# A hybrid decoder step: attention scores from 32-row products, another order of the projection's column groups, low halves of weights by an adding transfer

## The chip, the core and the metric

The kernel runs on one core of one Trainium2 chip. The metric is the device time of one launch in microseconds (us). Engines are named as in the profile: PE (TensorE, matmuls), DVE (VectorE), ACT (ScalarE), POOL (GpSimd), SP (the engine that issues most DMAs).

## What is computed

Two layers, each a mixing sub-layer and a feed-forward sub-layer, for 512 prompt rows and 32 sample rows (8 sequences of 4, over a paged cache of 2048 keys). All in float32. Cut from the reference, the mixing sub-layer:

```
P = rms_norm(x, g) @ w_in          # 1024 -> 2048: a, gate, u, v(sgu), q, k, v, d: 256 columns each
A: h = a*sigmoid(gate); causal depthwise conv, width 31; LayerNorm; silu        -> ya
B: u * (tril(W_s) @ (LN(v)*g + b) + b_s), chunks of 128, 4 heads (gelu on u, v)  -> yb
C: 4 heads, two softmax maps each of 32-wide keys/queries with ALiBi:
   p = softmax(q1 k1' + bias) - lam * softmax(q2 k2' + bias);  p @ v; RMSNorm    -> yc
D: means over windows 2/4/8/16 minus the token, a linear map per group           -> yd
x = x + rms_norm([ya yb yc yd] @ w_out)
```

## The kernel before

**Exact products.** Float32 products are made of three reduced-precision ones: every operand is split into a rounded high part and the rest, and hi·hi, lo·hi and hi·lo are accumulated. For a block of weights the high part `whi` is an ACT copy (L190) of the raw block, and the low part `wlo` is a DVE subtraction (L193), 128 x 1024 each. `whi` and `wlo` have rings of four slots, the raw blocks of 1 MB (256 columns) two.

**The projection.** `mixing` (L348) is run once a layer. It goes through eight column groups in the order of the table `order`; each is two chunks of 128 columns, and each chunk is done in two parts, the first 256 prompt rows and then 256 more with the 32 sample rows (288), 24 matmuls a part (8 blocks of the inner dimension times three products). `LAG` = 2: the second part of a chunk is written two steps after its first. So a layer has 8 x 2 x 2 x 24 = 768 such matmuls. The order before is a, gate, k, q, v, d, u, v of the gating: columns 0, 256, 1280, 1024, 1536, 1792, 512, 768.

**The mixers** are Python generators that are advanced between the projection's steps:

- `conv` with `taps` (A): once `gate` is there, DVE makes h (L410, tile `hext`) and then 31 instructions of 128 x 512 for each of the two chunks (L413 and 30 times L416, tile `cacc`), 60 at L416 a layer; then a LayerNorm over transposed tiles, a tanh, and the split into `ya` (L345 on ACT, L346 on DVE).
- `attention` (C): for each of two chunks 8 units, each with two score maps of width W = 128, 256, 384 or 512. Score products need k and q stacked as hi, lo, hi against hi, hi, lo in 96 rows, so that one matmul does all three products. `stack` builds these: a split of k and q (L474 on DVE), and 24 DMAs of 64 KB a chunk on SP (L478). DVE scales and takes the maximum of each map (L501), ACT takes the exponential, DVE makes the factors (L511 reciprocal, L512) and combines both maps (L513), PE transposes (L516) and multiplies with v (tile `oT`). It ends with an RMS norm on POOL and DVE and the split into `yc`.
- `gating` (B): LayerNorm per 128 tokens (L595), times gain (L596) plus offset (L597) as 128 x 256 tiles, and the product with W_s; `pooling` (D) ends with `yd`.

**The output product** (w_out, 192 matmuls of 512 columns in `project_last`) takes its inner blocks in the order `W_OUT_ORDER` = yd, ya, yb, yc. A Tile framework with a scheduler decides the order of the instructions on each engine when the program is built; each engine then runs its list in order.

Of the kernel before, what the change touches and what calls it, by code (L numbers as in the profile page):

```python
# [8 lines left out]
F32 = mybir.dt.float32  # L9
# [8 lines left out]
SEQ = 512  # L18
# [20 lines left out]
PB = 10  # L39
# [81 lines left out]
def trunk(ctx, tc, A, O):  # L121
# [15 lines left out]
    def acc():  # L137
        return psx("acc")
# [12 lines left out]
    ident = cst[:, C_ID:C_ID + 128]  # L151
    selkg = cst[:, C_KG:C_KG + 32]
# [123 lines left out]
    def params(l, tp, bank):  # L276
        lam_init = 0.8 - 0.6 * math.exp(-0.3 * l)
        rows = tp.tile([72, 128], F32, tag="prow", name="prow")
        for i, n in enumerate(("conv_b", "conv_ln_g", "conv_ln_b", "pool_scale")):
            SY.dma_start(rows[2 * i:2 * i + 2, :], A[n][l].rearrange("(c p) -> c p", p=128))  # L280
        SY.dma_start(rows[8:70, :], A["conv_w"][l].rearrange("t (c p) -> (t c) p", p=128))
        for i in range(2):
            SY.dma_start(rows[70:71, 64 * i:64 * i + 64], A["attn_sub_g"][l:l + 1, :])
        o = psx(bank)
        T.transpose(o[:, :71], rows[:71, :], ident[:71, :71])
        pf, lm = PF[l][0], PL[l]
        V.tensor_copy(pf[:, :71], o[:, :71])
        V.tensor_scalar(pf[:, 72:76], pf[:, 2:6], 0.5, None, op0=ALU.mult)
# [59 lines left out]
    def mixing(l, mp, early):  # L348
# [10 lines left out]
        kT, kh, kl, qh, ql = {}, {}, {}, {}, {}  # L359
# [33 lines left out]

        qT = {}
# [28 lines left out]
        def conv():  # L423
# [7 lines left out]
            cn = mp.tile([128, 256], F32, tag="t256", bufs=1, name="cn")  # L431
# [25 lines left out]
        ST = {}  # L457

        def stack():
            for c in range(2):  # L460
                st = ST[c] = {}

                o = ps()
                for t in range(4):
                    T.transpose(o[:, 128 * t:128 * t + 128], kT[c][:, 128 * t:128 * t + 128], ident)
                kt = mp.tile([128, 4, 128], F32, tag="t512", bufs=4, name="ktok")
# [3 lines left out]
                for nm, src, seqs in (("k", kT[c], (0, 1, 0)), ("q", qT[c], (0, 0, 1))):  # L470
                    hi = mp.tile([128, SEQ], F32R, tag="t512", bufs=4, name="qkh")
                    lo = mp.tile([128, SEQ], F32R, tag="t512", bufs=4, name="qkl")
                    S.copy(hi, src)
                    V.tensor_tensor(lo, src, hi.bitcast(F32), op=ALU.subtract)  # L474
                    s = yp.tile([128, 4, SEQ], F32R, tag="y", name=f"st_{nm}")
                    for jj in range(4):
                        for g in range(3):
                            SY.dma_start(s[32 * g:32 * g + 32, jj, :].bitcast(F32), (hi, lo)[seqs[g]][32 * jj:32 * jj + 32, :].bitcast(F32))  # L478
                    st[nm] = s
                    yield  # L480

        def attention():
            pb = mp.tile([128, SEQ], F32, tag="pb", name="pb")
            SY.dma_start(pb, A["c_pbias"])
            y = None
            for c in range(2):
                st = ST[c]
# [5 lines left out]
                def scores(i, hh):  # L493
                    h, W = 2 * c + hh, 128 * (i + 1)
                    P = []
                    for m in range(2):
                        sp = psx("s")
                        mm(sp[:, :W], st["q"][0:96, 2 * hh + m, 128 * i:128 * i + 128], st["k"][0:96, 2 * hh + m, 0:W])
                        p = mp.tile([128, SEQ], F32, tag="p", bufs=PB, name="p")
                        mn = mp.tile([128, 1], F32, tag="mn", bufs=8, name="mn")  # L500
                        V.tensor_tensor_reduce(p[:, :W], sp[:, :W], pb[:, SEQ - W:], SLOPES[h], 3.0e38,  # L501
                                               ALU.add, ALU.min, mn)
                        S.activation(p[:, :W], p[:, :W], AF.Exp, scale=-1.0, bias=mn, accum_out=den[:, i, hh, m:m + 1])
                        P.append(p)
                    Pm[i, hh] = P

                def weights(i, hh):
# [3 lines left out]
                    V.reciprocal(dn[:, 2:3], dn[:, 1:2])  # L511
                    V.tensor_scalar(dn[:, 3:4], dn[:, 0:1], dn[:, 2:3], nlam, op0=ALU.mult, op1=ALU.mult)  # L512
# [15 lines left out]
                for u in range(len(units) + UL):  # L528
                    if u < len(units):
                        scores(*units[u])  # L530
                    if u >= UL:
                        i, hh = units[u - UL]
                        weights(i, hh)
                        if hh == 1:
                            values(i)
                    yield
                os_ = mp.tile([128, SEQ], F32, tag="t512", bufs=4, name="os_")
                sq = mp.tile([128, SEQ], F32, tag="t512", bufs=4, name="sq")
# [12 lines left out]
                rb = mp.tile([128, 4, 2, 64], F32, tag="t512", bufs=4, name="rb")  # L551
# [12 lines left out]
        def gating():  # L564
            wn = mp.tile([128, 4, 128], F32, tag="t512", bufs=4, name="wn")
# [17 lines left out]
            SG[l] = (wc, bc)  # L583
            yield
# [5 lines left out]
            for t in range(4):  # L590
# [5 lines left out]
                V.tensor_tensor(vn[:, t, :], vn[:, t, :], gr[:, 0, :], op=ALU.mult)  # L596
                V.tensor_tensor(vn[:, t, :], vn[:, t, :], gr[:, 1, :], op=ALU.add)  # L597
                yield
            y = yp.tile([128, 2, 2, SEQ], F32R, tag="y", name="yb")
            for c in range(2):  # L600
                o = acc()
                for n in range(4):
                    for hh in range(2):
# [3 lines left out]
                V.tensor_tensor(t, o.rearrange("p (n t) -> p n t", n=4),  # L607
                                bsg[:, c:c + 1, :].to_broadcast([128, 4, 128]), op=ALU.add)
# [9 lines left out]
        def pooling():  # L618
# [7 lines left out]
            cn = mp.tile([128, 256], F32, tag="t256", bufs=1, name="cn")  # L626
# [57 lines left out]
        def load(c0):  # L684
# [4 lines left out]
            else:  # L689
                pairs[c0] = raw_cols(w, c0, V, early.get(c0), None, G if c0 == 0 and early else None)  # L690
# [21 lines left out]
        for u in range(n + LAG):  # L712
# [17 lines left out]
            if b >= 0:  # L730
# [14 lines left out]
                if c0 == 1024 and i == 1:  # L745
                    active.append(stack())
                if i == "v":
                    active.append(attention())
# [635 lines left out]
    with tc.tile_pool(name="pro", bufs=1, reuse_waits="tile") as pro, \  # L1384
# [76 lines left out]
```

## Time and profile before

| | |
|---|---|
| time, median of 3 runs | 1456.01 us (1452.26 to 1457.11) |
| the profiled execution | 1448.71 us, of it 1446.8 us from the first to the last instruction |
| PE, DVE, ACT, POOL busy | 95%, 57%, 35%, 18% of the span |
| the first layer's mixing | 14 to 175 us; its w_out from 175 us |
| the second layer's mixing | 736 to 890 us; its w_out from 890 us |

Busy shares are means over the whole span; the two mixing stages are about a fifth of it, and there DVE is busier than its mean. The granted clock is 1.00 (2.4 GHz) in most stretches and 0.50 (1.2 GHz) in some.

### The profile page before, as it was taken

To read this page: it belongs to the slowest core of one execution; us is meant where nothing else is said; L and a number is where in the kernel's file an instruction comes from. 1 tells how busy PE (TensorE), PEld (TensorE's weight loads), DVE (VectorE), ACT (ScalarE), POOL (GpSimd) and SP (SyncE) were. 2 spreads that over 40 slices of the span, in tenths; PEclk is the share of its full clock that TensorE was granted. 3 is DMA by queue.
4 is the path that set the end of the run, shared out by engine and by line. 5 is a ranking of instruction groups with operands and counts; after the bars stand their busy time and mean duration, and the time that the engine had idled before them with its cause. 6 is when DMAs were issued, how large, how long until landed. Compare 5 with 4: busy or idle time off the path is not lost.

```text
span 1446.8 us, 22864 instructions
## 1 busy us (share of the span) xinstructions
PE 1372.0 (95%) x9114; PEld 1078.7 (75%) x9114; DVE 823.8 (57%) x1660; ACT 504.7 (35%) x985; POOL 262.7 (18%) x271
## 2 busy tenths in 40 slices
PE   6999787999999999999989988989999999999997
PEld 6987576877666777777689976777776677768775
DVE  4986759866434333333669976778663333333344
ACT  4346634322224321222343474543322332222231
POOL 1000145455300000000220011544442000000003
PEclk9999799999999999999999997999999999999999
DMA  6452134888848752132434521468877496213132
GB/s 206 116 156 73 59 121 145 301 307 297 296 164 254 241 171 77 59 117 106 150 120 119 146 68 58 163 237 281 318 276 266 153 315 220 81 61 114 59 135 91
DMA packets 160091, 242.15 MB, mean 167 GB/s; under 512 B 10444, under 2 KB 118226, under 8 KB 159986
## 3 DMA queue, kind: packets, MB, share of 16 engines
q1 hardware_dynamic: 141410, 173.32, 37.1%
q0 software_dynamic: 18432, 67.12, 12.4%
q8 instruction: 72, 1.18, 0.3%
q14 instruction: 33, 0.27, 0.1%
q10 hardware_dynamic: 144, 0.26, 0.0%
HBM read 222.33 MB, written 12.04 MB: 162 GB/s over the span
## 4 chain that ended last, share of the span: by engine, by line
PE 81%; DVE 11%; ACT 2%; DMA 2%; issue 2%; POOL 1%; SPq 1%; DVEq 0%; POOLq 0%; ACTq 0%
PE acc L126 61%; PE sx L126 12%; PE ps L126 3%; DVE sca L872 2%; PE s L126 1%; DVE cacc L416 1%; DVE p L501 1%; DVE wlo L193 1%; DVE m L1301 1%; PE oT L126 1%; DVE x_t L1294 1%; ACT whi L190 1%; PE ps L516 1%; SPq L478 1%; PE ps L1001 1%
## 5 line engine op out<-in xcount | busy, mean ns | idle before, releaser
L126 PE MATMUL acc<-xhi,whi 128*128 128x512 f32 (+2 forms) x1152 | 405.5, 353 | 3.2 <-ACT whi L190 2.0
L126 PE MATMUL acc<-xhi,wlo 128*128 128x512 f32 (+2 forms) x1152 | 403.4, 351 | 0.2 <-DVE wlo L193 0.2
L126 PE MATMUL acc<-xlo,whi 128*128 128x512 f32 (+2 forms) x1152 | 402.0, 349 | 1.3 <-DVE xlo L238 1.3
L190 ACT CAST whi<-raw 128x1024 fp32r<-128x1024 f32 x178 | 184.3, 1048 | 333.7 <-PE acc L126 292.8
L193 DVE TENSOR_TENSOR wlo<-raw,whi 128x1024 fp32r<-128x1024 f32 x172 | 217.1, 1268 | 128.7 <-ACT whi L190 126.8
L126 PEld LDWEIGHTS acc<-xhi,whi 128*128 128x128 f32 x1152 | 217.1, 189 | 42.2 <-issue 8.0
L126 PEld LDWEIGHTS acc<-xlo,whi 128*128 128x128 f32 x1152 | 217.2, 189 | 31.9 <-issue 4.1
L126 PEld LDWEIGHTS acc<-xhi,wlo 128*128 128x128 f32 x1152 | 216.9, 188 | 31.5 <-issue 4.7
L126 PE MATMUL acc<-whi,h 128*128 128x512 f32 x704 | 226.7, 397 | 0.0
L126 PEld LDWEIGHTS acc<-whi,h 128*128 128x128 f32 x704 | 131.2, 188 | 44.1 <-issue 11.1
L126 PE MATMUL acc<-wlo,h 128*128 128x512 f32 x352 | 138.6, 395 | 0.0
L1276 POOL TENSOR_TENSOR m<-m,g_g_ffn_post 128x512 f32<-128x512 f32 x14 | 20.1, 1437 | 504.9 <-ACT junk L1275 504.9
L989 DVE STREAM_TRANSPOSE kt<-kr 128x1024 f32<-128x1024 f32 x64 | 78.5, 1233 | 27.6 <-DMA kr<-in_cache_k_dram,ik 23.3
L986 POOL DMA_INDIRECT kr<-in_cache_k_dram,ik x64 | 73.8, 1154 | 100.1 <-DVE kt L989 72.2
L416 DVE SCALAR_TENSOR_TENSOR cacc<-hext,pf,cacc 128x512 f32<-128x512 f32 x120 | 85.4, 747 | 0.6
L1345 DVE SCALAR_TENSOR_TENSOR th<-th,acc 128x512 f32<-128x512 f32 (+1 forms) x46 | 29.9, 649 | 87.2 <-PE acc L126 87.0
L126 PEld LDWEIGHTS acc<-wlo,h 128*128 128x128 f32 x352 | 66.1, 188 | 17.6 <-issue 4.5
L174 POOL TENSOR_TENSOR rsw<-rsw,mhalf 128x1 f32<-128x1 f32 (+2 forms) x62 | 39.1, 636 | 202.9 <-DVE rsw L173 189.4
L1016 POOL DMA_INDIRECT vr<-in_cache_v_dram,iv x64 | 63.2, 988 | 57.0 <-PE sx L126 41.2
L1154 DVE SCALAR_TENSOR_TENSOR sth<-sth,ps 128x64 f32<-128x64 f32 x22 | 4.8, 220 | 86.5 <-ACT sth L1153 86.5
L550 POOL TENSOR_TENSOR rse<-e,mhalf 128x8 f32<-128x8 f32 x4 | 8.5, 2130 | 242.7 <-DVE e L548 242.7
L126 PE MATMUL sx<-vr,pt 128*32 128x256 f32 x512 | 49.3, 381 | 0.0
(401 smaller groups left out, 1864.8 us busy)
## 6 DMA issues: line engine op xcount, KB each, us to landing
raw<-in_w_gu_dram SPq DMA_DIRECT2D x44, 1024.0 KB
raw<-in_w_down_dram SPq DMA_DIRECT2D x20, 1024.0 KB
rws<-in_w_gu_dram SPq DMA_DIRECT2D x40, 512.0 KB
raw<-in_w_in_dram SPq DMA_DIRECT2D x16, 1024.0 KB
raw<-in_w_out_dram SPq DMA_DIRECT2D x8, 1024.0 KB
rwo<-in_w_out_dram SPq DMA_DIRECT2D x16, 512.0 KB
rws<-in_w_down_dram SPq DMA_DIRECT2D x16, 512.0 KB
x<-x_t SPq DMA_DIRECT2D x12, 512.0 KB
```

What stands on the lines that cost most here:

```text
L126: T.matmul(out, lhsT, rhs, start=start, stop=stop)
L174: G.tensor_tensor(y, v, mhalf[:P, :n], op=ALU.pow)
L190: S.copy(hi, src)
L193: eng.tensor_tensor(lo, src, hi.bitcast(F32), op=ALU.subtract)
L416: V.scalar_tensor_tensor(a, hext[c][:, t:t + SEQ], pf[:, 8 + 2 * t + c:9 + 2 * t + c], a, op0=ALU.mult, op1=ALU.add)
L478: SY.dma_start(s[32 * g:32 * g + 32, jj, :].bitcast(F32), (hi, lo)[seqs[g]][32 * jj:32 * jj + 32, :].bitcast(F32))
L872: V.scalar_tensor_tensor(a[:, c], ext[:, c, :, t:t + 4], pf[:, 8 + 2 * t + c:9 + 2 * t + c], a[:, c], op0=ALU.mult, op1=ALU.add)
L986: G.indirect_dma_start(out=kr, out_offset=None, in_=ck, in_offset=bass.IndirectOffsetOnAxis(ap=ik[:, s, bg:bg + 1], axis=0))
L989: V.transpose(kt, kr)
L1016: G.indirect_dma_start(out=v.rearrange("p t e -> p (t e)"), out_offset=None, in_=cv, in_offset=bass.IndirectOffsetOnAxis(ap=iv[:, s, a:a + ...
L1276: (V if (t, half) == (3, 1) else G).tensor_tensor(m[t][:, hs], m[t][:, hs], gain[:, hs], op=ALU.mult)
L1345: V.scalar_tensor_tensor(th[:, :n], th[:, :n], 0.5, ou[:, :n], op0=ALU.mult, op1=ALU.mult)
```

## The change

- **Order of the groups:** k, q, v first, then a, gate, u, v of the gating, d last. `attention` starts when the first chunk of q is done, and no longer waits for stacks.
- **Scores:** no stacks (48 DMAs, 4 DVE splits and 8 transposes a layer fall away). High and low parts of k and q are made where the projection's result is read (`ev_qk`: 8 DVE instructions of 256 columns a layer instead of 4 of 512), and each map is three accumulated matmuls over 32 rows. The keys go out through 16 small products with a unit matrix.
- **Low halves:** in the five groups a, gate, u, v of the gating and d, ACT writes -raw rounded into `wlo`, a GpSimd DMA that adds in place puts the raw weights on top from memory (512 KB, runs of 512 bytes), and ACT makes `whi`: 10 such transfers a layer in place of 10 DVE subtractions.
- **Small ones:** reciprocals and factors for both maps' units of a pair at once (16 + 16 become 8 + 8); gain and offset of the gating's LayerNorm move behind the product with W_s (8 DVE instructions fewer, four matmuls and one DVE instruction more); `PB` (score tiles) 10 to 8, ring `t512` 4 to 3.

```diff
-PB = 10
+PB = 8
+    identr = cp.tile([128, 128], F32R, name="identr")
+    S.copy(identr, ident)
...
+        qk = {(nm, c): [mp.tile([128, SEQ], F32R, name=f"{nm}{c}{s}") for s in "hl"] for nm in "kq" for c in range(2)}
...
+        def ev_qk(nm, c, f):
             def ev(o, half):
+                hi, lo = qk[nm, c]
                 hs = slice(256 * half, 256 * half + 256)
+                if nm == "k":
+                    S.copy(hi[:, hs], o[:, :256])
+                    V.tensor_tensor(lo[:, hs], o[:, :256], hi[:, hs].bitcast(F32), op=ALU.subtract)
                 else:
+                    sc = cst[:, C_QS + c:C_QS + c + 1]
+                    S.activation(hi[:, hs], o[:, :256], AF.Copy, scale=sc)
+                    V.scalar_tensor_tensor(lo[:, hs], o[:, :256], sc, hi[:, hs].bitcast(F32), op0=ALU.mult, op1=ALU.subtract)
...
         order = [
+            (1280, [(10, ev_qk("k", 0, 10)), (11, ev_qk("k", 1, 11))]),
+            (1024, [(8, ev_qk("q", 0, 8)), (9, ev_qk("q", 1, 9))]),
+            (1536, "v"),
             (0, [(0, ev_copy(hext[0], 0, 0.5, 30)), (1, ev_copy(hext[1], 1, 0.5, 30))]),
             (256, [(2, ev_ga(0)), (3, ev_ga(1))]),
-            (1280, [(10, ev_tmp(kT, 0, 10, "kT")), (11, ev_tmp(kT, 1, 11, "kT"))]),
-            (1024, [(8, ev_tmp(qT, 0, 8, "qT")), (9, ev_tmp(qT, 1, 9, "qT"))]),
-            (1536, "v"),
-            (1792, [(14, ev_copy(dext[0], 14, 1.0, 15)), (15, ev_copy(dext[1], 15, 1.0, 15))]),
             (512, [(4, ev_copy(uv[:, 0], 4)), (5, ev_copy(uv[:, 1], 5))]),
             (768, [(6, ev_copy(uv[:, 2], 6)), (7, ev_copy(uv[:, 3], 7))]),
+            (1792, [(14, ev_copy(dext[0], 14, 1.0, 15)), (15, ev_copy(dext[1], 15, 1.0, 15))]),
         ]
...
+        def keys_out():
             for c in range(2):
                 o = ps()
                 for t in range(4):
+                    for s in range(2):
+                        mm(o[:, 128 * t:128 * t + 128], qk["k", c][s][:, 128 * t:128 * t + 128], identr, start=(s == 0), stop=(s == 1))
...
+                    sps = [psx("s") for _ in range(2)]
+                    for n, (a, b) in enumerate(((0, 0), (0, 1), (1, 0))):
+                        for m in range(2):
+                            r = slice(64 * hh + 32 * m, 64 * hh + 32 * m + 32)
+                            mm(sps[m][:, :W], qk["q", c][a][r, 128 * i:128 * i + 128], qk["k", c][b][r, 0:W], start=(n == 0), stop=(n == 2))
                     for m in range(2):
-                        sp = psx("s")
-                        mm(sp[:, :W], st["q"][0:96, 2 * hh + m, 128 * i:128 * i + 128], st["k"][0:96, 2 * hh + m, 0:W])
+                        sp = sps[m]
...
-                V.tensor_tensor(vn[:, t, :], vn[:, t, :], gr[:, 0, :], op=ALU.mult)
-                V.tensor_tensor(vn[:, t, :], vn[:, t, :], gr[:, 1, :], op=ALU.add)
...
-                pairs[c0] = raw_cols(w, c0, V, early.get(c0), None, G if c0 == 0 and early else None)
+                if c0 in (1280, 1024):
+                    pairs[c0] = raw_cols(w, c0, V, early.get(c0), None, G if c0 == 1280 and early else None)
+                    return
+                r = raw_load(w, c0)
+                pairs[c0] = []
+                for i in range(2):
+                    hi = wp.tile([128, 8, 128], F32R, tag="whi", bufs=4, name="whi")
+                    lo = wp.tile([128, 8, 128], F32R, tag="wlo", bufs=4, name="wlo")
+                    src = r[:, :, 128 * i:128 * i + 128]
+                    S.activation(lo, src, AF.Copy, scale=-1.0)
+                    G.dma_start(lo, w[:, c0 + 128 * i:c0 + 128 * i + 128].rearrange("(k p) f -> p k f", p=128),
+                                accum_op=ALU.add)
+                    S.copy(hi, src)
+                    pairs[c0].append((hi, lo))
...
+                if c0 == 1024:
+                    done.add(("q", i))
+                    if i == 0:
+                        active.append(attention())
+                    else:
+                        active.append(keys_out())
                 if i == "v":
-                    active.append(attention())
+                    done.add("v")
```

How the instructions stand on three engines' lists, in the first layer (numbers behind names tell copies of a tile apart; line numbers are those of each kernel).

DVE, before, where the convolution begins; `wlo` are low halves of weights, `hext` is h, `cacc` the convolution's sum:

```order
L193 TENSOR_TENSOR wlo<-raw,whi 128x1024
L410 SCALAR_TENSOR_TENSOR hext_231<-tg,hext_231 128x512
L296 TENSOR_TENSOR lam_81<-lam_81 128x1
L582 COPY bc_1814<-bsg 128x8
L413 TENSOR_SCALAR cacc_442<-hext_231,pf_82 128x512
L297 TENSOR_SCALAR lam_81<-lam_81 128x1
L416 SCALAR_TENSOR_TENSOR cacc_442<-hext_231,pf_82,cacc_442 128x512 x4
L193 TENSOR_TENSOR wlo<-raw,whi 128x1024
L416 SCALAR_TENSOR_TENSOR cacc_442<-hext_231,pf_82,cacc_442 128x512 x6
```

The same place of the change (`p,mn<-s,pb` is a score map with its maximum):

```order
L499 ISA p,mn<-s,pb 128x256
L499 ISA mn 128x1
L419 SCALAR_TENSOR_TENSOR hext_233<-tg,hext_233 128x512
L499 ISA p,mn<-s,pb 128x256
L499 ISA mn 128x1
L422 TENSOR_SCALAR cacc_1216<-hext_233,pf_84 128x512
L425 SCALAR_TENSOR_TENSOR cacc_1216<-hext_233,pf_84,cacc_1216 128x512
L499 ISA p,mn<-s,pb 128x256
L499 ISA mn 128x1
L425 SCALAR_TENSOR_TENSOR cacc_1216<-hext_233,pf_84,cacc_1216 128x512 x2
```

The first instruction on `hext` stood at row 26 of DVE's list, ahead of all score maps, and stands at row 98, behind 22 of the layer's 32 maps.

DVE, before, the rows around the last low half of `yc`, the last operand of w_out to be made:

```order
L597 TENSOR_TENSOR vn<-vn,sgr 128x256
L607 TENSOR_TENSOR uv<-acc,bsg 128x512 x2
L610 TENSOR_TENSOR uv<-uv 128x512 x2
L346 TENSOR_TENSOR yb<-uv,yb 128x512 x2
L548 SCALAR_TENSOR_TENSOR e_1984<-ps,e_1984 128x8
L552 COPY rb<-rse 128x512
L556 SCALAR_TENSOR_TENSOR os__1975<-os__1975,pf_82,ps 128x512
L346 TENSOR_TENSOR yc<-os__1975,yc 128x512
```

The end of the mixing on DVE in the change:

```order
L350 TENSOR_TENSOR yb<-uv,yb 128x512
L652 TENSOR_TENSOR s_1917<-wn,cst 128x15
L653 SCALAR_TENSOR_TENSOR wn<-wn,cst,dext_236 128x497
L175 TENSOR_SCALAR rsw<-ag 128x1
L655 TENSOR_TENSOR wn<-s_1917,dext_236 128x15
L450 TENSOR_SCALAR xn<-ps,ag,rsw 128x256
L350 TENSOR_TENSOR yd<-wn,yd 128x512
L460 SCALAR_TENSOR_TENSOR cacc_1216<-hext_233,cacc_1216 128x512
L460 SCALAR_TENSOR_TENSOR cacc_1722<-hext_234,cacc_1722 128x512
L350 TENSOR_TENSOR ya<-cacc_1216,ya 128x512
L350 TENSOR_TENSOR ya<-cacc_1722,ya 128x512
```

The last operand to be made was `yc`; now `yc` is made far ahead, and `ya` is the last, right behind `yd` and `yb`.

POOL, before, from the clearing of the convolution's margins on:

```order
L355 MEMSET hext_231 128x30
L356 MEMSET dext_233 128x15
L355 MEMSET hext_232 128x30
L356 MEMSET dext_234 128x15
L550 TENSOR_TENSOR rse<-e_1534,mhalf 128x8
L578 AFFINE_SELECT wt<-wt 128x512
```

And in the change:

```order
L359 MEMSET hext_234 128x30
L360 MEMSET dext_236 128x15
L703 DMA wlo<-in_w_in_dram 128x8x128 x7
L552 TENSOR_TENSOR rse<-e_1084,mhalf 128x8
L703 DMA wlo<-in_w_in_dram 128x8x128 x3
L552 TENSOR_TENSOR rse<-e_1574,mhalf 128x8
```

Ten adding transfers stand on POOL's list, around the first of the two instructions (`rse`) on which attention's norm waits.

## Rows read from the trace of the kernel before

**Rows 1.** The profile page: busy time of the engines, and the chain that ended last.

```profile
PE 1372.0 (95%) x9114; PEld 1078.7 (75%) x9114; DVE 823.8 (57%) x1660; ACT 504.7 (35%) x985; POOL 262.7 (18%) x271
...
PE 81%; DVE 11%; ACT 2%; DMA 2%; issue 2%; POOL 1%; SPq 1%; DVEq 0%; POOLq 0%; ACTq 0%
```

**Rows 2.** Windows: PE, PEld, DVE, ACT, POOL busy (x); PE clock; DMA share, GB/s.

```profile
175.00:188.50 13.50, 12.02 (x64) 9.93 (x60) 5.14 (x10) 3.10 (x6) 2.19 (x3) 1.00 0.03 11
188.50:223.00 34.50, 32.09 (x151) 25.21 (x151) 25.81 (x91) 13.00 (x31) 15.74 (x14) 1.00 0.46 155
223.00:245.00 22.00, 15.92 (x91) 13.55 (x91) 21.87 (x49) 12.41 (x27) 13.67 (x13) 0.84 0.47 152
40.42:122.15 81.73, 78.33 (x606) 74.22 (x604) 76.44 (x153) 37.06 (x93) 0.00 (x0) 1.00 0.46 130
122.15:188.48 66.33, 52.05 (x331) 42.05 (x327) 40.11 (x121) 37.79 (x78) 11.76 (x13) 0.82 0.16 53
149.90:170.40 20.50, 12.68 (x47) 8.20 (x47) 16.37 (x58) 14.98 (x33) 4.00 (x6) 0.50 0.15 52
```

**Rows 3.** DVE's instructions by line, 40.4 to 188.4 us.

```profile
L416 DVE SCALAR_TENSOR_TENSOR cacc<-hext,pf,cacc 128x512 f32<-128x512 f32 x60 | 42.6, 747 | 0.3
L193 DVE TENSOR_TENSOR wlo<-raw,whi 128x1024 fp32r<-128x1024 f32 x15 | 18.6, 1238 | 2.8 <-ACT whi L190 2.7
L501 DVE CUSTOM_DVE_ANT_0 p<-s,pb 128x128 f32<-128x128 f32 (+3 forms) x32 | 14.8, 482 | 1.8 <-PE s L126 1.7
L513 DVE SCALAR_TENSOR_TENSOR p<-p,den 128x128 f32<-128x128 f32 (+3 forms) x16 | 8.4, 543 | 0.1
L512 DVE TENSOR_SCALAR den<-den,lam 128x1 f32<-128x1 f32 x16 | 4.0, 266 | 0.1
...
L596 DVE TENSOR_TENSOR vn<-vn,sgr 128x256 f32<-128x256 f32 x4 | 1.6, 421 | 0.0
...
L474 DVE TENSOR_TENSOR qkl<-kT,qkh 128x512 fp32r<-128x512 f32 x2 | 1.4, 688 | 0.7 <-DMA st_q<-qkh 0.7
```

**Rows 4.** The chain of waits, 36 to 66 us: start, us, what.

```profile
47.43 3.07 PE acc L126 x23
...
59.11 2.65 DVE cacc L416 x4
```

**Rows 5.** DVE's timeline: first gating multiply, a last tap, last low half, both layers.

```profile
40.42 0.68 DVE L410 SCALAR_TENSOR_TENSOR hext<-tg,hext 128x512 f32<-128x512 f32 x1
...
113.39 0.75 DVE L416 SCALAR_TENSOR_TENSOR cacc<-hext,pf,cacc 128x512 f32<-128x512 f32 x1
...
188.48 0.69 DVE L346 TENSOR_TENSOR yc<-os__1975,yc 128x512 fp32r<-128x512 f32 x1 [0.68 <-ACT yc L345]
...
759.62 0.68 DVE L410 SCALAR_TENSOR_TENSOR hext<-tg,hext 128x512 f32<-128x512 f32 x1
...
903.59 0.69 DVE L346 TENSOR_TENSOR yc<-os__8388,yc 128x512 fp32r<-128x512 f32 x1 [0.68 <-ACT yc L345]
```

**Rows 6.** PE's timeline at four places, with what it waited for.

```profile
37.94 0.23 PE L285 MATMUL ps<-cst,prow 71*128 71x71 f32 x1
...
188.50 0.50 PE L126 MATMUL acc<-whi,yc 128*128 128x512 f32 x1 [1.49 <-ACT yc L345]
...
192.29 0.50 PE L126 MATMUL acc<-whi,yd 128*128 128x512 f32 x1 [2.13 <-ACT whi L190]
...
268.49 0.28 PE L126 MATMUL acc<-xhi,whi 128*128 128x256 f32 x1
268.61 0.28 PE L126 MATMUL acc<-xlo,whi 128*128 128x256 f32 x1
268.82 0.53 PE L126 MATMUL sx<-kt,qs 128*32 128x128 f32 x11
```

**Rows 7.** GpSimd's gathering transfers of the paged keys (512 KB each): duration, landing.

```profile
L986 POOL DMA_INDIRECT kr<-in_cache_k_dram,ik x64: 933/941/1936, 252.2 to 1086.2; - x64
...
DMA to landing us min/median/max: 4.2/6.5/9.8
```

More of the change, by code (lines that the diff above doesn't have):

```diff
@@ L277, in params @@
         lam_init = 0.8 - 0.6 * math.exp(-0.3 * l)
-        rows = tp.tile([72, 128], F32, tag="prow", name="prow")
+        rows = tp.tile([74, 128], F32, tag="prow", name="prow")
         for i, n in enumerate(("conv_b", "conv_ln_g", "conv_ln_b", "pool_scale")):
@@ L283, in params @@
             SY.dma_start(rows[70:71, 64 * i:64 * i + 64], A["attn_sub_g"][l:l + 1, :])
+        SY.dma_start(rows[71:73, :], A["sgu_ln_g"][l].rearrange("(c p) -> c p", p=128))
         o = psx(bank)
-        T.transpose(o[:, :71], rows[:71, :], ident[:71, :71])
+        T.transpose(o[:, :73], rows[:73, :], ident[:73, :73])
         pf, lm = PF[l][0], PL[l]
         V.tensor_copy(pf[:, :71], o[:, :71])
+        V.tensor_copy(pf[:, 77:79], o[:, 71:73])
         V.tensor_scalar(pf[:, 72:76], pf[:, 2:6], 0.5, None, op0=ALU.mult)
@@ L358, in mixing @@
         vtok = mp.tile([128, 4, 256], F32, name="vtok")
-        kT, kh, kl, qh, ql = {}, {}, {}, {}, {}
+        qk = {(nm, c): [mp.tile([128, SEQ], F32R, name=f"{nm}{c}{s}") for s in "hl"] for nm in "kq" for c in range(2)}
+        pb = mp.tile([128, SEQ], F32, name="pb")
+        SY.dma_start(pb, A["c_pbias"])
+        done = set()
         tg = {}
@@ L454, in conv @@
             Y[0] = y
-        ST = {}
-        def stack():
+        def keys_out():
             for c in range(2):
-                st = ST[c] = {}
                 o = ps()
                 for t in range(4):
-                    T.transpose(o[:, 128 * t:128 * t + 128], kT[c][:, 128 * t:128 * t + 128], ident)
-                kt = mp.tile([128, 4, 128], F32, tag="t512", bufs=4, name="ktok")
+                    for s in range(2):
+                        mm(o[:, 128 * t:128 * t + 128], qk["k", c][s][:, 128 * t:128 * t + 128], identr, start=(s == 0), stop=(s == 1))
+                kt = mp.tile([128, 4, 128], F32, tag="t512", bufs=3, name="ktok")
                 S.copy(kt, o.rearrange("p (t f) -> p t f", t=4))
@@ L469, in stack @@
                 yield
[L470 to L480, printed above, removed]
         def attention():
-            pb = mp.tile([128, SEQ], F32, tag="pb", name="pb")
-            SY.dma_start(pb, A["c_pbias"])
             y = None
             for c in range(2):
-                st = ST[c]
+                while ("q", c) not in done:
+                    yield
                 oT = psx("oT")
@@ L510, in weights @@
                     dn = den[:, i, hh]
-                    V.reciprocal(dn[:, 2:3], dn[:, 1:2])
-                    V.tensor_scalar(dn[:, 3:4], dn[:, 0:1], dn[:, 2:3], nlam, op0=ALU.mult, op1=ALU.mult)
+                    if hh == 0:
+                        d2 = den[:, i]
+                        V.reciprocal(d2[:, :, 2:3], d2[:, :, 1:2])
+                        V.scalar_tensor_tensor(d2[:, :, 3:4], d2[:, :, 0:1], nlam, d2[:, :, 2:3], op0=ALU.mult, op1=ALU.mult)
                     V.scalar_tensor_tensor(P[0][:, :W], P[1][:, :W], dn[:, 3:4], P[0][:, :W], op0=ALU.mult, op1=ALU.add)
@@ L534, in attention @@
                         if hh == 1:
+                            while "v" not in done:
+                                yield
                             values(i)
                     yield
-                os_ = mp.tile([128, SEQ], F32, tag="t512", bufs=4, name="os_")
-                sq = mp.tile([128, SEQ], F32, tag="t512", bufs=4, name="sq")
+                os_ = mp.tile([128, SEQ], F32, tag="t512", bufs=3, name="os_")
+                sq = mp.tile([128, SEQ], F32, tag="t512", bufs=3, name="sq")
                 S.copy(os_, oT)
@@ L583, in gating @@
             SG[l] = (wc, bc)
+            o = acc()
+            for h in range(4):
+                mm(o[64 * (h % 2):64 * (h % 2) + 64, 128 * (h // 2):128 * (h // 2) + 128], gr[:, 64 * h:64 * h + 64], wt[:, h, :])
+            V.tensor_tensor(bsg, o[:, :256].rearrange("p (c t) -> p c t", c=2), bsg, op=ALU.add)
             yield
@@ L606, in gating @@
                 t = uv[:, 2 + c, :].rearrange("p (n t) -> p n t", n=4)
[L607 to L608 removed]
+                V.scalar_tensor_tensor(t, o.rearrange("p (n t) -> p n t", n=4), pf[:, 77 + c:78 + c],
+                                       bsg[:, c:c + 1, :].to_broadcast([128, 4, 128]), op0=ALU.mult, op1=ALU.add)
                 tf = uv[:, 2 + c, :]
@@ L1391, in trunk @@
         g = grow(pro, "g_mix_pre", 0)
-        early = {0: raw_load(A["w_in"][0], 0)}
+        early = {1280: raw_load(A["w_in"][0], 1280)}
         for t in range(2, 5):
             SY.dma_start(xs[t][:rows_of(t)], x_at(0)(128 * t, rows_of(t)))
-        early[256] = raw_load(A["w_in"][0], 256)
+        early[1024] = raw_load(A["w_in"][0], 1024)
         for t in range(5):
```

26 lines of the change are left out of this document (8 added, 18 removed).

## The prediction

> **What bounds the kernel now.** The page first: PE is busy 95% of the span, and the chain that ended last runs over PE for 81% and over DVE for 11% [rows 1]. Over the whole kernel, a us taken from DVE is therefore worth nothing where PE is full. So the stages have to be looked at one by one, and the windows show three of them in a layer's mixing [rows 2]. From 40.4 to 122.2 us both engines are full (PE 78.3, DVE 76.4 of 81.7 us). From 122.2 to 188.5 neither is (52.1 and 40.1 of 66.3); here the stage waits for chains of small steps, and PE's clock falls to 0.50, its lower level of 1.2 GHz, for 20.5 us in which it is busy for 12.7. Then the output product fills PE again (32.1 of 34.5 us). The timeline shows what releases it: the product's matmul at 188.50 waited for `yc`, whose low half DVE made at 188.48 [rows 5, 6]. So the end of the mixing is set by the mixer that is made last, and a change in this stage is worth what it does to that moment, S. The change makes another mixer last (`ya`), so S has to be built anew: when can the convolution begin (T0), how much DVE work stands from there to the last `ya`, and how much of w_out is left at that moment.
>
> **T0, where the convolution can begin.** Before, DVE multiplies the gate into h at 40.42 [rows 5]. After, `a` and `gate` are the fourth and fifth groups. I counted PE's list: the transpose of the parameters, at 37.94 before [rows 6], has the same 184 matmuls ahead of it in both kernels. Behind it, up to the second part of the gate's first chunk, stand 240 projection matmuls of 256 columns, 120 of 288, 66 of scores (22 maps, three each, 279 columns on average), 16 that bring out keys, and some 40 transposes and products with v. Prices: 0.12 us for 256 columns (268.49 to 268.61, [rows 6]), 0.133 for 288 (23 in 3.07 us, [rows 4]), so 0.46 ns a column. That makes 28.8 + 16.0 + 8.5 + 1.8 + 6.6 (the last an estimate at 0.11 to 0.2 each) = 61.7, and with 0.7 for the tanh on ACT T0 = 37.9 + 61.7 + 0.7 = 100.3. Three corrections:
>
> - A score product uses 32 of the array's rows, and changes its tiling and back. Where the kernel before changes from full size to 32 columns, the next start comes after 0.21 us and not after 0.12 [rows 6]: 0.09 each way. There are 13 bursts before T0: +2.4 us. The Trainium skill (TensorEngine Tiling, Key Properties) says that a change of the tiling mode drains the engine; the trace agrees by these 0.09 us.
> - The two maps of a unit lie in different rows of the array and are written alternately. If such pairs run side by side, half of 8.5 us falls away; if not, nothing. No row of before shows a product of 32 rows. I take half of it, -2.2 us.
> - The adding transfers. No row shows one. Nearest are the gathered keys, of the same size and also issued by POOL: 4.2 to 9.8 us to landing, 6.5 in the middle [rows 7]. Low end 4.2. They move 128 pieces of 4 KB and the adding transfer 1,024 pieces of 512 bytes, so the high end is 9.8 plus seven more issues of 0.94 = 16. Counting on PE's list from the matmul that frees a slot of the ring to the first that reads the new weights, less an ACT pass, the slack is 7.2 us for the first chunk of `a`, 8.7 for the second, 4.9 for the first of the gate. At 6.5 only the last is late, by 1.6 us. The Trainium skill (DMA: Bandwidth & Descriptors, Anatomy of one DMA) gives 2.0 us plus the bytes at 436 KB a us, an estimate of 3.2 us here; the gathered keys take twice that, so I stay with the rows.
>
> T0 = 100.3 + 2.4 - 2.2 + 1.6 = 102, which is 62 us later than before. Ends: 96 and 118.
>
> **DVE from T0 to the last `ya`.** Before, from the first multiply to the last low half, DVE is busy 76.4 + 40.1 = 116.6 us [rows 2]. What of it is gone or lies ahead of T0 in the change (neighbours overlap by 0.08 us: four taps in 2.65 us, 0.66 each against 0.75 by itself [rows 3, 4]; it is taken off each):
>
> - 22 of 32 score maps lie ahead; the ten left have 4,096 of 10,240 columns, so 60% of 14.8 goes, less overlap: 7.1.
> - Ten of 16 combinations (L513) lie ahead; the rest has 45% of the columns: 3.8. Factors: 26 small instructions at 0.19 and half of that: 3.4.
> - 4 low halves of weights are left of 15: 11 x 1.16 = 12.8. Splits of k and q (L474): 2.4. Gain and offset (L596 and its twin): 2.7, less 0.4 for the new addition [rows 3].
>
> Together 31.8, so 85 us stay, in which the 60 taps alone are 40. The relief is real, about 16 us a layer over the whole stage, but before T0 DVE now has only about 38 us of work, and an engine can't catch up later what it was not given earlier. About 65 us of the 85 stand up to the last tap. Taps are always at hand, so this runs between gapless (65) and the 93.5% of the window from 40.4 [rows 2] (69.5); I take 67. The 20 us behind it (pooling, both layer norms, gating, `yd`, `yb`, `ya`) are a chain through PE, POOL, ACT and DVE as in the window from 122.2, where DVE works 60% of the time [rows 2]: 20 if gapless, 33 at that rate. Part of the chain overlaps with the taps; I take 26.
>
> S = 102 + 67 + 26 = 195, against 188.5 before. Ends: 96 + 85 = 181, and 118 + 102 = 220.
>
> **What it costs at the end.** PE is done with the projection some 53 us behind T0 and waits for S, with w_out behind it. Before, 49 of w_out's 192 matmuls had run while it waited (most of the 64 in the window from 175 [rows 2]); from 188.5 on, 143 x 0.23 us (512 columns at 0.46 ns) = 32.9 and a stall of 2.1 at 192.29 [rows 6] ended at 223.5. After the change only six matmuls stand ahead of `ya` in PE's list: 186 x 0.23 = 42.8, and 195 + 42.8 = 237.8: +14.3. In layer 1 the multiply is 719.2 us later and the last `yc` at 903.59, that is 184.4 on the first layer's scale [rows 5]; the same sum gives +18.4. These hold where PE sets the end. Behind w_out DVE is full (21.9 of 22 us from 223 to 245 [rows 2]), and if its list sets the end, only the shift of S counts: +6.5 and +10.6. So between +17 and +33; I take the middle, **+24**. Nothing is gained elsewhere: the 48 DMAs, the splits and the transposes lay in a stretch where PE was full with projections, and 64 more score matmuls a layer fall into the same. ACT's ten additional copies find it half idle (37 of 82 us [rows 2]). The half clock comes with any long wait of PE; it is there before and will be after: 0, with up to 3 us a layer in the range.
>
> The profiled execution took 1448.7 us, the median run 1456.0: 1473 on the first, **1480** on the second.
>
> **The rivals.**
>
> - *The adding transfers land late.* At 12 us the three chunks ahead of T0 are late by 4.8, 3.3 and 7.1, so T0 = 116, 14 us more a layer: +52, 1508. At 16 us +75. For it: eight times as many pieces as any row. Against it: memory is only half used in this stretch (0.46 [rows 2]). The Trainium skill (SBUF — State Buffer, the "DVE blocks DMA" trap) holds that descriptors of such transfers wait while DVE runs in its fast two-port modes; that would act here too, and would make this case; no row shows it.
> - *Faster.* The taps run gapless, the tail hides in them, and the score pairs run side by side: T0 = 96 to 98, S = 181 to 183. PE's end then moves by 0 to +2 and by +4 to +6, and if DVE sets the end, S moves by -7 and -3: about -6, 1450. The point at which it decides is S = 181 in layer 0 and 177 in layer 1. For it: DVE has 16 us less work a layer. Against it: PE's list alone puts T0 at 96 or later.
> - *No change*: S about 184, the shifts cancel: within 4.4 us.
>
> **How the numbers follow.** Late taps as worked out 0.52 (1464 to 1500), transfers late 0.22 (1495 to 1545), faster 0.17 (1440 to 1451), no change 0.09. 0.3% or 4.4 us is about what a measurement can tell (the three runs lie within 4.9 us). The range takes 1450 to 1522 and leaves out the upper part of the second case and most of the third. Faster 0.17, same 0.09, slower 0.74.
>
> **What would show it.** The first multiply into `hext` near 102 us (near 822 in layer 1) shows T0; later than 112 with PE waiting for `wlo` would be the transfers; `wlo`'s landing time decides. Taps gapless from there to about 169, and `ya`'s low half near 195. PE's first `ya` matmul waiting for it, with about 20 us or more of waiting ahead. If `ya` comes before 181, or w_out's order lets much more than six matmuls run ahead of it, the forecast is wrong.

## The result

The change is slower: median 1516.05 us (1513.65 to 1520.91) against 1455.99 (1452.26 to 1457.11), ratio 1.042 with a 95% interval of 1.040 to 1.044, +60 us. The forecast was 1480: the direction and the range held, the size was off by a factor of 2.5. The forecast had the mechanism only in part.

The page of the change; its engines' busy time and the chain that ended last answer to [rows 1]:

```profile
PE 1421.7 (94%) x9274; PEld 1109.0 (73%) x9274; DVE 798.7 (53%) x1604; ACT 510.4 (34%) x992; POOL 295.6 (20%) x291
...
PE 80%; DVE 9%; DMA 4%; issue 3%; ACT 2%; POOL 2%; SPq 0%; DVEq 0%; POOLq 0%; ACTq 0%
```

DVE did lose 25 us of work, as the change meant it to. The span grew by 68.1 us all the same (the two profiled executions lie a little further apart than the medians). What is new in the chain is DMA, 4% after 2%.

Where the 68 us lie: the clearing of the convolution's margins (`hext` on POOL) opens a layer's mixing. In before, from the view of the tile `hext` behind 700 us:

```profile
L355 POOL MEMSET hext<- x2: 131/131/131, 745.7 to 745.8; 128x30 f32 x2
```

In the change:

```profile
L359 POOL MEMSET hext<- x2: 129/130/130, 775.4 to 775.5; 128x30 f32 x2
```

So layer 0 costs 29.7 us, and what follows the opening of layer 1 the remaining 38.4. Most of both lies in the mixing, as its last operands show. DVE's timeline of the change answers to [rows 5]:

```profile
107.80 0.69 DVE L419 SCALAR_TENSOR_TENSOR hext<-tg,hext 128x512 f32<-128x512 f32 x1
...
178.78 0.74 DVE L425 SCALAR_TENSOR_TENSOR cacc<-hext,pf,cacc 128x512 f32<-128x512 f32 x1
...
207.82 0.69 DVE L350 TENSOR_TENSOR yd<-wn,yd 128x512 fp32r<-128x512 f32 x1 [3.60 <-ACT yd L349]
...
209.80 1.30 DVE L350 TENSOR_TENSOR ya<-cacc,ya 128x512 fp32r<-128x512 f32 x2
...
862.83 0.69 DVE L419 SCALAR_TENSOR_TENSOR hext<-tg,hext 128x512 f32<-128x512 f32 x1
...
964.36 1.29 DVE L350 TENSOR_TENSOR ya<-cacc,ya 128x512 fp32r<-128x512 f32 x2
```

The first multiply comes at 107.8 (forecast 102), the last low half of `ya` starts at 210.4 (195); it is the second of the two in the line that begins at 209.80. Against the last `yc` of before that is 21.9 us in layer 0; in layer 1 it is 965.0 - 903.6 = 61.4, of which 29.7 came with it, so 31.7. The windows of these stretches answer to [rows 2], with a short one, 86.4 to 97, to which the text comes below:

```profile
37.94:107.80 69.86, 65.03 (x496) 58.54 (x495) 17.57 (x69) 33.59 (x86) 9.55 (x6) 0.95 0.59 118
107.80:178.80 71.00, 58.61 (x404) 51.17 (x403) 62.93 (x120) 31.28 (x70) 13.70 (x8) 0.90 0.42 82
178.80:210.40 31.60, 20.46 (x92) 13.33 (x93) 20.75 (x52) 9.31 (x18) 4.50 (x9) 0.72 0.34 111
...
86.40:91.00 4.60, 1.56 (x13) 1.19 (x13) 0.00 (x0) 0.38 (x1) 0.89 (x1) 0.86 1.44 185
91.00:97.00 6.00, 6.00 (x31) 6.00 (x30) 0.00 (x0) 0.38 (x1) 0.00 (x0) 0.54 0.23 30
```

What is to be seen: up to 107.8 DVE is busy for 17.6 of 69.9 us; from there to the end of `ya` for 62.9 + 20.8 = 83.7 of 102.6. The work was forecast at 85 and is 83.7. The rest are gaps in DVE's work, 19 us, and these were forecast at 8.

### The profile page after: what moved, and what is told of

It reads as the page before. It is cut to its first block, busy times and chain, and to the rows that moved or that the text cites. A ratio compares the mean times of both kernels' runs of the same rounds, so it can differ in the third digit from the quotient of the medians.

```text
span 1514.9 us, 23026 instructions
## 1 busy us (share of the span) xinstructions
PE 1421.7 (94%) x9274; PEld 1109.0 (73%) x9274; DVE 798.7 (53%) x1604; ACT 510.4 (34%) x992; POOL 295.6 (20%) x291
## 3 DMA queue, kind: packets, MB, share of 16 engines
q0 software_dynamic: 39232, 77.60, 17.7%
## 4 chain that ended last, share of the span: by engine, by line
PE 80%; DVE 9%; DMA 4%; issue 3%; ACT 2%; POOL 2%; SPq 0%; DVEq 0%; POOLq 0%; ACTq 0%
PE acc L126 61%; PE sx L126 11%; PE ps L126 3%; PE s L126 2%; DVE sca L892 2%; DMA wlo<-in_w_in_dram 2%; DVE wlo L195 1%; DVE x_t L1314 1%; DVE m L1321 1%; DMA raw<-in_w_in_dram 1%; POOL rsw L176 1%; PE oT L126 1%; PE ps L1021 1%; PE ps L237 1%; DVE xlo L240 1%
## 5 line engine op out<-in xcount | busy, mean ns | idle before, releaser
L126 PE MATMUL acc<-xhi,whi 128*128 128x512 f32 (+2 forms) x1152 | 414.1, 360 | 8.4 <-DVE vn L600 5.8
L126 PE MATMUL acc<-xhi,wlo 128*128 128x512 f32 (+2 forms) x1152 | 412.4, 358 | 10.1 <-DMA wlo<-in_w_in_dram 9.9
L126 PE MATMUL acc<-xlo,whi 128*128 128x512 f32 (+2 forms) x1152 | 411.3, 357 | 1.3 <-DVE xlo L240 1.1
L192 ACT CAST whi<-raw 128x1024 fp32r<-128x1024 f32 x158 | 163.8, 1048 | 345.6 <-PE acc L126 292.8
L126 PEld LDWEIGHTS acc<-xhi,whi 128*128 128x128 f32 x1152 | 225.2, 196 | 50.6 <-issue 9.0
L126 PEld LDWEIGHTS acc<-xhi,wlo 128*128 128x128 f32 x1152 | 224.8, 195 | 45.7 <-DMA wlo<-in_w_in_dram 11.0
L195 DVE TENSOR_TENSOR wlo<-raw,whi 128x1024 fp32r<-128x1024 f32 x152 | 191.7, 1268 | 126.1 <-ACT whi L192 121.0
L126 PEld LDWEIGHTS acc<-xlo,whi 128*128 128x128 f32 x1152 | 225.0, 195 | 34.1 <-issue 6.1
L499 DVE CUSTOM_DVE_ANT_0 p<-s,pb 128x128 f32<-128x128 f32 (+3 forms) x64 | 29.6, 487 | 101.0 <-PE s L126 100.9
L126 PEld LDWEIGHTS acc<-wlo,h 128*128 128x128 f32 x352 | 66.1, 188 | 17.7 <-issue 4.5
L1036 POOL DMA_INDIRECT vr<-in_cache_v_dram,iv x64 | 62.9, 982 | 55.4 <-PE sx L126 39.5
L1365 DVE SCALAR_TENSOR_TENSOR th<-th,acc 128x512 f32<-128x512 f32 (+1 forms) x46 | 29.7, 646 | 81.7 <-PE acc L126 81.3
L703 POOL DMA_DIRECT2D wlo<-in_w_in_dram x20 | 31.5, 1577 | 199.0 <-ACT wlo L702 119.7
```

Source lines behind the costliest of these rows:

```text
L126: T.matmul(out, lhsT, rhs, start=start, stop=stop)
L195: eng.tensor_tensor(lo, src, hi.bitcast(F32), op=ALU.subtract)
L703: G.dma_start(lo, w[:, c0 + 128 * i:c0 + 128 * i + 128].rearrange("(k p) f -> p k f", p=128), accum_op=ALU.add)
L1036: G.indirect_dma_start(out=v.rearrange("p t e -> p (t e)"), out_offset=None, in_=cv, in_offset=bass.IndirectOffsetOnAxis(ap=iv[:, s, a:a + ...
L1365: V.scalar_tensor_tensor(th[:, :n], th[:, :n], 0.5, ou[:, :n], op0=ALU.mult, op1=ALU.mult)
```

## The experiments

Every kernel was timed beside the kernel before on its chip, so the ratios compare; 0.01 is 14.6 us. Differences in us below are worked out from the ratios. Three theories are set against each other. Theory O, also called D: the convolution starts late, and DVE's work behind the gate sets the end. Theory T: the adding transfers do. Theory P: PE's list does, in which the last projections stand behind steps of the gating. "Kernel 3" is the kernel of experiment 3. Kernels 6, 8 and 10 leave out 15 of the 31 taps and so compute another convolution.

**1. All low halves on DVE, nothing else changed.**

```diff
-                if c0 in (1280, 1024):
+                if c0 != 1536:
```

> The change with all low halves of weights subtracted on DVE as before, no adding transfer. Theory O (the order: the convolution starts 67 us late and DVE has too little to do until then): the convolution still starts late, at about 100 us instead of 107.8, four more low halves a layer lie behind it; 1495 to 1512 us. Theory T (the adding transfers: PE waits for them and their stall costs the clock): most of the 60 us come back, 1455 to 1475 us.

Ratio 1.041 (1.038 to 1.044), 1512 us: the same as the change. T falls as the sole cause. The edit weighs the transfers against ten subtractions a layer that DVE gets back (1.2 us each); it does not price them alone. The start and the end say more, in DVE's timeline and in one window of this kernel:

```profile
101.63 0.69 DVE L419 SCALAR_TENSOR_TENSOR hext<-tg,hext 128x512 f32<-128x512 f32 x1
...
208.10 0.69 DVE L350 TENSOR_TENSOR yd<-wn,yd 128x512 fp32r<-128x512 f32 x1 [3.60 <-ACT yd L349]
210.09 1.29 DVE L350 TENSOR_TENSOR ya<-cacc,ya 128x512 fp32r<-128x512 f32 x2
...
101.63:210.70 109.07, 81.39 (x492) 66.72 (x492) 87.98 (x181) 39.87 (x85) 12.49 (x13) 0.80 0.20 64
```

The convolution begins 6.2 us earlier, and `ya` ends at the same time. DVE has 4.3 us more to do behind that start (88.0 against 83.7), four low halves, so its list by itself would have ended 1.9 us earlier. The gaps are 21 us instead of 19: they, and not only the start and the amount of DVE's work, make that end. In front of `ya` stands `yd`, which waits 3.6 us for ACT, here as in the change.

**2. The order of before, low halves on DVE:** the 32-row scores and the small edits are what is left (a and gate are loaded early, as before). Of the edit, the order alone, shortened:

```diff
+            (0, ...), (256, ...),
             (1280, ...), (1024, ...), (1536, "v"),
-            (0, ...), (256, ...), (512, ...), (768, ...), (1792, ...),
+            (1792, ...), (512, ...), (768, ...),
```

> The change with the order of the groups of before (a, gate, k, q, v, d, u, v of the gating) and all low halves on DVE; what is left are the 32-row scores without stacks and the small edits. Theory O: first multiply near 41 us, 1430 to 1456 us, 45 us or more below the run with the new order and the same low halves. Theory T: the same as that run within 10 us.

Ratio 1.000 (0.998 to 1.002). With equal low halves the order is worth 58 us, all of the loss. As Theory O expected.

**3. The same order with adding transfers for d, u and v of the gating**, six a layer:

```diff
-                if c0 != 1536:
+                if c0 in (0, 256, 1280, 1024):
```

> The order of before, with adding transfers for the three groups d, u and v of the gating alone (six a layer). Theory O: DVE is relieved of six low halves (7 us) in its full stretch; within 10 us of the run with the old order and DVE's low halves, rather below. Theory T: each landing of 7 to 11 us holds PE, 15 us or more above it.

Ratio 1.015 (1.012 to 1.018), 21 us above kernel 2: as Theory T expected, and Theory O missed this one. The transfers do cost here, where PE is full (13.0 of 13.0 us from 95 to 108). In this kernel's chain of waits, 104 to 202 us, and in PE's waits from 40 to 200 us:

```profile
107.88 0.81 PE ps L516 x6
108.80 11.83 DMA wlo<-in_w_in_dram
120.68 4.41 PE acc L126 x22
...
PE acc L126 <- DMA wlo<-in_w_in_dram: 5.0, 2, 2.5
```

Nearly all of the loss is in the first layer: the second mixing opens at 765.2 us and in kernel 2 at 745.7, while the whole spans differ by 23.2. How 5 us of waiting became 19 was not taken apart, so the 21 us are not a price per transfer.

**4. w_out's blocks in the order yc, yb, yd, ya** (`W_OUT_ORDER` = 4, 5, 2, 3, 6, 7, 0, 1).

> The change with the output product's blocks in the order yc, yb, yd, ya, so that more of it can run while the convolution is unfinished. If PE sets the end of w_out (as the prediction's upper sum has it, six matmuls ahead instead of 49): 6 to 10 us less a layer, 1496 to 1504 us. If DVE's list sets it: 1510 to 1518 us.

Ratio 1.041 (1.038 to 1.044), not told apart from the change. w_out now starts at 171 us and not at 197, the last low half of `ya` starts at 206.0, and the last product at 254.6, 49 us behind; in the change 51 us behind. What of w_out runs ahead of the last operand was not worth the 12 to 20 us that the count of products had promised.

**5. d ahead of u and of v of the gating**, in the change: the order is k, q, v, a, gate, d, u, v of the gating. **6. 16 of 31 taps**, in the change. **7. v behind the gate**, in the change: the order is k, q, a, gate, v, u, v of the gating, d. **8. 16 of 31 taps** in kernel 2. The edit of 6, which 8 has too:

```diff
-            for t in range(1, CW):
+            for t in range(1, CW, 2):
...
-                if t % 2 == 0:
+                if t % 4 == 3:
```

> The change with d projected ahead of u and v of the gating instead of last. Theory D (DVE's work of 84 us behind the late gate sets the end): nothing is taken from that list, 1508 to 1518 us. Theory P (PE's list does: the last products of d stand behind steps of the gating that wait for DVE, and pooling is late by that): pooling is done early, 8 us or more a layer, at most 1500 us.

Kernel 5: ratio 1.030 (1.028 to 1.032), 18 us less than the change: P has a share. The window from the first multiply to the last low half shows it:

```profile
108.45:202.70 94.25, 72.98 (x497) 60.52 (x497) 83.39 (x170) 40.60 (x88) 16.31 (x17) 0.90 0.39 87
```

The start and DVE's work are those of the change (108.5 and 83.4 us), and the end comes 7.7 us earlier, because the gaps are 11 us instead of 19.

> The change with 16 of the convolution's 31 taps (every second one from the third on is left out, so the convolution isn't the reference's): 30 DVE instructions, 20 us a layer, less behind the gate. Theory D: nearly all of it comes back, 1472 to 1484 us. Theory P: at most a quarter, 1505 us or more.

Kernel 6: ratio 1.025 (1.023 to 1.027), 25 us less, between the two theories. The timeline shows why. `ya` is done 30 us earlier, and pooling's `yd` has taken its place as the last:

```profile
179.74 1.29 DVE L350 TENSOR_TENSOR ya<-cacc,ya 128x512 fp32r<-128x512 f32 x2
...
200.63 0.69 DVE L350 TENSOR_TENSOR yd<-wn,yd 128x512 fp32r<-128x512 f32 x1 [2.05 <-ACT yd L349]
```

> The change with v projected behind a and gate instead of ahead of them: the convolution can begin 120 matmuls or 14 us earlier. Theory D: the time follows the start, 1486 to 1498 us. Theory P: 1508 us or more.

Kernel 7: ratio 1.030 (1.028 to 1.033), 17 us less, 1500 us on the scale of 1456 and so just above what D expected. The start came 16 us earlier, at 91.4, the end of `ya` only 7.

> The same 16 of 31 taps in the kernel with the order of before and DVE's low halves (whose time is that of before). If the taps lie beside other work there, as the windows of before say of the stretch from 122 us on, at most 10 us come back: 1443 to 1456 us. If taps cost their time in either order, 1415 us.

Kernel 8: ratio 1.012 (1.009 to 1.016), slower by 17 us than kernel 2 with all taps; neither theory had that. `ya` is done at 113 instead of 169 us and nothing is won by it, since attention and the gating are last in this order (in kernel 2 `yc` comes at 180.8 and `yb` at 183.4). That attention's `yc` then comes at 192.5 was not expected. With fewer steps of the convolution the generators take turns otherwise and the lists differ; which rows of them cost the 12 us was not settled.

**9. v behind the gate and d ahead of u. 10. 16 of 31 taps and d ahead of u. 11. The kernel before with the small edits alone.**

> The change with v behind the gate and d ahead of u: order k, q, a, gate, v, d, u, v of the gating. Each move alone gave about 18 us. If the two limits (the convolution's late start, pooling's late end) stand one behind the other, both moves add up: 1474 to 1486 us on the scale where before is 1456 (ratio to before about 1.017). If they are the same slack, no more than one of them: ratio 1.026 or more.

Kernel 9: ratio 1.030 (1.027 to 1.032), no more than either move alone. `yd` is early (161.6), the convolution starts at 91.7, and `ya` still ends at 201.6.

> 16 of 31 taps (the convolution isn't the reference's) with d ahead of u. With 16 taps alone the convolution was done at 180 us in layer 0 and pooling at 201, so pooling took over as the last. If that is why only 25 us came back, taps and d together give 45 us or more: ratio 1.01 or less. If something else holds the end, ratio 1.02 or more.

Kernel 10: ratio 1.017 (1.015 to 1.018), 37 us less than the change, more than either alone, but 8 us short of what was expected for both together. In its trace the gating has become last: `yb` comes at 193.3 us, `ya` at 185.0.

> The kernel before with the small edits alone (factors of softmax for a pair at once, gain and offset of the gating's LayerNorm behind the product), stacks, order and low halves as before. They take 8 + 16 small DVE instructions a layer, about 5 us. In the old order DVE is not the last at the end: 0 to 6 us less, ratio 0.996 to 1.0. If it is faster by more than the kernel with old order, 32-row scores and the same edits (ratio 1.000), then the 32-row scores cost what lies between.

Kernel 11: ratio 0.997 (0.996 to 0.998), 1451.9 us, the fastest version, 0.3% ahead of the kernel before. Kernel 2, which has the 32-row scores and the shorter rings in addition, is some 5 us slower: they gain nothing.

**12. Kernel 9 with all low halves on DVE** (the edit of 1).

> The order k, q, a, gate, v, d, u, v of the gating with all low halves on DVE. With the adding transfers this order gave ratio 1.030, and its projection ended at 171 us in layer 0. If what held it there were the transfers (in the old order six of them a layer cost 21 us, because PE is full where they land), the ratio falls to 1.010 to 1.018. If DVE's late taps hold it, the four or more low halves that come back to DVE make it 1.028 or more.

Ratio 1.010 (1.008 to 1.012). Without the transfers kernel 9 gains 29 us, although DVE gets ten low halves a layer back. In this kernel the first multiply is at 84.9, and the ends in DVE's timeline are these:

```profile
151.60 0.68 DVE L350 TENSOR_TENSOR yd<-wn,yd 128x512 fp32r<-128x512 f32 x1
...
176.84 0.69 DVE L350 TENSOR_TENSOR yc<-os__1843,yc 128x512 fp32r<-128x512 f32 x1
...
189.81 1.29 DVE L350 TENSOR_TENSOR ya<-cacc,ya 128x512 fp32r<-128x512 f32 x2
```

The 14 us that are left above kernel 2 are found in S: behind its layer's opening the last low half starts at 170.4 and 164.2 us, in kernel 2 at 163.6 and 157.6.

Side by side, ratios to before:

| order of the groups | adding transfers | low halves on DVE |
|---|---|---|
| k, q, v, a, gate, u, v(gating), d (the change) | 1.042 | 1.041 |
| d ahead of u | 1.030 | - |
| v behind the gate | 1.030 | - |
| both | 1.030 | 1.010 |
| a, gate, k, q, v, d, u, v(gating) (before) | 1.015 (six a layer) | 1.000 |

Three limits stand beside each other: the late gate, the late d, and the transfers. Each one hides another: the first that is taken away gives 0 (transfers) to 18 us (the late d), and the transfers give 29 once the other two are gone.

## Why the prediction was wrong

**Right: T0 without the transfers.** 100.3 from PE's list, less up to 4.4 and plus 2.4 for the scores, is 98.3; kernel 1 has 101.6. Both corrections can be read in PE's timeline of the change, where two maps of 256 columns are written:

```profile
44.18 0.28 PE L126 MATMUL acc<-whi,xlo 128*128 128x256 f32 x1
44.39 0.39 PE L126 MATMUL s<-k0h,q0h 32*128 32x256 f32 x2
44.62 0.28 PE L126 MATMUL s<-k0l,q0h 32*128 32x256 f32 x2
44.73 0.27 PE L126 MATMUL s<-k0h,q0l 32*128 32x256 f32 x2
44.94 0.40 PE L126 MATMUL acc<-xhi,whi 128*128 128x288 f32 x1
```

Into the scores the start is 0.21 us apart and out of them 0.21, against 0.12 between equals: the 0.09 of the forecast each way. The third pair follows the second after 0.11 us, the price of one product: pairs in different rows do run side by side, fully, where I had taken half. Behind the first pair the next starts after 0.23 us, 0.11 more; that I had not, and it is 1.4 us for 13 bursts. The Trainium skill (TensorEngine Tiling (Array Packing), Tiling Modes, Key Properties) says that different tiles can execute in parallel; the trace agrees by this 0.11.

**Wrong, first: the price of a transfer** in T0 (1.6 us of waiting). The chain of waits of the change, 40 to 130 us:

```profile
50.90 7.67 DMA wlo<-in_w_in_dram
...
79.07 11.36 DMA wlo<-in_w_in_dram
```

The issues of the pair in POOL's timeline, and the window of the second one:

```profile
77.18 1.54 POOL L703 DMA_DIRECT2D wlo<-in_w_in_dram  x1 [16.71 <-ACT wlo L702]
79.07 1.54 POOL L703 DMA_DIRECT2D wlo<-in_w_in_dram  x1 [0.35 <-ACT vs L716]
...
79.07:90.44 11.37, 8.37 (x69) 7.48 (x68) 0.51 (x4) 5.39 (x12) 3.08 (x2) 0.97 1.23 210
```

Alone it takes 7.7 us, near the 6.5 that I took; the second of a pair, issued 1.9 us after the first, takes 11.4, and for pairs I had no term. DVE was busy for 0.51 of these 11.4 us, so DVE's work can hardly have held the second one up. (The estimate of 3.2 us from the Trainium skill, DMA: Bandwidth & Descriptors, Anatomy of one DMA, is less than half of the one alone: the measurement decides.) PE stood 3.0 us (window 86.4 to 91) and then ran 6 us at a clock of 0.54, close to its lower level of 1.2 GHz. T0 was 5.8 us late by that, and 6.2 us earlier without transfers. In the change this is hidden, as kernel 1 shows; it becomes 21 and 29 us in kernels 3 and 9, where I take PE's list to be the next limit.

**Wrong, second, and the main one: the tail.** I took 67 us to the last tap and 26 behind it; measured are 71 and 31.6, with DVE's work as forecast: what was mis-sized are its gaps. I had PE "done with the projection some 53 us behind T0", at 155, and looked for no wait of it before w_out. PE's timeline shows it waiting inside the projection:

```profile
166.17 1.12 PE L126 MATMUL acc<-wt,sgr 128*64 128x128 f32 x8 [3.04 <-POOL wt L579]
...
178.91 0.61 PE L126 MATMUL acc<-xhi,whi 128*128 128x288 f32 x1 [4.46 <-DVE vn L600]
179.32 0.44 PE L126 MATMUL acc<-xlo,whi 128*128 128x288 f32 x1
179.56 0.44 PE L126 MATMUL acc<-xhi,wlo 128*128 128x288 f32 x1
```

The last part of d does not read `vn`; it waits for the accumulator that the gating's `vn` (L600) on DVE has to read first, and DVE is then in the backlog of taps. That part starts at 179, runs at half pace at first (0.24 us a matmul instead of 0.133), and pooling, which needs it, ends at 208, just ahead of `ya` on DVE. So the late convolution delays d through PE's list, and d delays the convolution's end through DVE's list. I counted each list by itself. The first product on `ya` did not wait for it, as the forecast's sign would have it; the wait is that for `yd`, the operand just ahead:

```profile
207.84 0.79 PE L126 MATMUL acc<-whi,yd 128*128 128x512 f32 x1 [2.25 <-ACT yd L349]
...
210.56 0.63 PE L126 MATMUL acc<-whi,ya 128*128 128x512 f32 x1
```

Kernel 5 shows the share of this link (18 us), and the taps give 25 alone (kernel 6) and 18 where that link is already gone (10 against 5).

**Wrong, third: the end.** I had w_out of before end at 223.5 on PE's count, and took the middle between that and "only the shift of S counts". In PE's timeline of before its last product starts here:

```profile
239.14 0.39 PE L126 MATMUL acc<-whi,yc 128*128 128x512 f32 x1
```

and in the change here:

```profile
261.78 0.63 PE L126 MATMUL acc<-whi,yc 128*128 128x512 f32 x1
```

22.6 us later for an S that is 21.9 later; kernel 4 points the same way. Before, 42 of the 192 products had started ahead of S, in the change 12: a lead of 30 products, 7 us of PE. Most of it went into waits behind S:

```profile
225.71 0.66 PE L235 MATMUL sx<-cst,m 128*128 128x128 f32 x4 [1.59 <-DVE m L1301]
229.79 1.11 PE L235 MATMUL sx<-cst,m 128*128 128x128 f32 x4 [3.43 <-DVE xlo L238]
230.56 0.78 PE L126 MATMUL acc<-wlo,yc 128*128 128x512 f32 x1
231.13 0.63 PE L126 MATMUL acc<-whi,yc 128*128 128x512 f32 x1
```

The last 26 products stand behind these waits, and the first of them run at half pace (0.43 us instead of 0.23). So the count of products was the wrong upper sum, and a look at where w_out ended in the trace of before would have refuted it. Another 7 us of layer 0 come behind w_out; they were not in the sum, and what causes them was not tried.

**Wrong, fourth: layer 1.** I put it on layer 0's scale by its first multiply. By the opening of the layer, its last `yc` came at 157.9 us (745.7 to 903.6) and layer 0's at 168.5 (20.0 to 188.5), so the lead of before is 10.6 us and not 4.1. S behind the opening is about the same after (191 and 190 us).

Added up in S alone: forecast 6.5 + 10.6, measured 21.9 + 31.7. Of the 15.4 us that layer 0 missed, 5.8 stand in T0, 4 in the stretch of the taps and 5.6 behind it. The rival "transfers late" had the right time (1508) and is not what happened: with no transfers the time is 1512. That its number is nearer is luck. The rival "faster" failed at its own point: S never came near 181. Two slips in the working left the forecast as it is: the upper end of T0, 118, fits 12 us a transfer and not to the 16 named as the high end, and the window's 0.46 is the share of the DMA engines, not of memory.

## What to carry to other kernels

Relief of an engine counts from the moment at which its work can begin: DVE lost 25 us here, and it was idle for 52 of the 70 us ahead of the gate. Where several engines run fixed lists, walk the lists together, row by row, past the first wait: a product that needs what another mixer's step has to free inherits its lateness. And when an edit that should have mattered gives nothing, repeat it after the next limit is gone, as with the transfers (1.042 against 1.041 in one order, 1.030 against 1.010 in another).

## What was not expected of the hardware

An adding transfer of 512 KB in runs of 512 bytes takes 7.7 us alone and 11 to 12 us as the second of a pair. By the two profile pages, the queue of software transfers went from 12.4% of 1446.8 us to 17.7% of 1514.9, with 20 adding transfers more: an estimate of 88.7 us of all 16 engines together, or 4.4 us each. Two at a time would need 8.8 us by that, more than the 7.7 of one alone. Its issue holds POOL for 1.55 us (64 gathers of the same size: 0.94 [rows 7]).
